# A hybrid encoder layer on one core: two gate chunks move from branch A's filler to the paired block products, and branch A's transposes and value products follow two steps later

## The chip, the core and the metric

The kernel runs on one core of a Trainium2 chip. Its engines are TensorE (PE in the profile, with weight loads as PEld), VectorE (DVE), ScalarE (ACT), GpSimd (POOL) and SyncE (SP), which here only issues DMA transfers. The metric is device microseconds (us) of one execution, as the median of several runs.

## What is computed

One encoder layer for two sequences, a prompt of 256 rows and a sample of 1024, together 1280 rows of width 1024 in float32.

```python
def _layer(x, rel_bias, g_mix, w_in, b_gate, w_branch_a, w_branch_b, w_out, sink, g_mlp, w_up, w_down):
    h = _rmsnorm(x, g_mix)
    z = h @ w_in
    # qa, ka, va | qb, kb, vb | gates: columns of z
    ...
    gates = jax.nn.sigmoid((z[..., o6:] + b_gate).astype(jnp.float32)).astype(x.dtype)
    gates = gates.reshape(b, S, 2, D_MODEL)
    o_a, _ = _banded_attention(qa, ka, va, A_WINDOW, 1, rel_bias[:, :A_HEADS], sink)
    o_b = _dilated_mixture(qb, kb, vb, rel_bias[:, A_HEADS:])
    merged = gates[:, :, 0] * (o_a.reshape(b, S, A_Q) @ w_branch_a) + gates[:, :, 1] * (o_b @ w_branch_b)
    x = x + merged @ w_out
    h = _rmsnorm(x, g_mlp)
    return x + jnp.square(jax.nn.relu(h @ w_up)) @ w_down
```

Branch A is attention in a window of 128 with 8 query heads, 2 key heads and a sink in the denominator. Branch B is a mixture of three dilated windows, weighted by a softmax over their log-sums. A final RMS norm follows the layer.

## The kernel before, in words

Every matrix product of float32 data is made of three: each operand is split in a high part (`whi`, `hhi`, made by an ACT copy) and a remainder (`wlo`, `hlo`, made by a DVE subtraction), and PE adds high × low, low × high and high × high.

The stages, in order of time. First the norm and the values' columns of `z`. Then 14 **pairs** (`PAIRS`, `pair()` L1039): two chunks of 128 columns of `w_in` are taken together, and their product with the sample's rows is made as seven products of blocks (`seven` L359) in place of eight, with the prompt's rows by a plain product (`prompt` L362). Pairs 0 to 8 run alone; pairs 9 to 13 (from `MIXED` on) run with branch B's attention beside them. The last six pairs hold gate columns, whose results are stored to DRAM (`scr_g`). Then comes **branch A's loop** (L1465), and then 48 merging **jobs** (the loop behind it), each of which multiplies branch B's or A's output with `w_branch_b` or `w_branch_a` and, on DVE, with a gate. `w_out` and the MLP end the kernel.

Branch A's loop runs over 40 tiles, four units (pairs of heads) of ten tiles of 128 rows, two tiles to a step `j`. A step of PE has, in this order: `values_of` (L1199) of the tiles four back, `transposes` (L1183) of the tiles two back, `scores` (L1160) of tile j, filler, scores of tile j+1, filler. DVE adds the bias and takes the maxima (L1170, L1174), ACT takes the exponentials (L1180), both copy the transposed weights out of PSUM (L270, L272), and DVE copies the result `o` (L1213), which SP stores.

The **filler** is the generator `logits()` (L1216). It makes the five gate chunks that are left (`PLAIN`), each as three plain products (512, 512 and 256 rows, `mm3` L188), with 24 matmuls each. It hands back control after 4 wide matmuls or 8 narrow ones; a step of the loop takes three such pieces. A result is copied by ACT (`gs`, L1227) and stored. The next chunk's weights are split (`prepare()`, `whi` L231, `wlo` L235) on the way.

Beside the loop, `merge()` (L1245) makes branch B's mixture on POOL (L1342, L1345) from rows `r` that SP loads (L1323, L1326), two items to a step. `wslot` hands out a ring of ten buffers (`N_W`) to all of `raw`, `whi`, `wlo`, `gs` and `r`; whoever takes a buffer waits for the last reader of what was there.

At the loop's end, `sums_a` (L1410 to L1413) turns the sums of exponentials into reciprocals; `rows_a` transposes them on PE (L1418), copies them (L1420) and stores them (L1422); `widen` (L1431) loads them back, spread over partitions. `fetch()` (L222) loads the next weights, `load_gate` (L1449) gates, `open_gate` (L1454) takes their sigmoid, and `high_b`, `low_b` (L1378, L1381) split branch B's output. A job's product lies in one of three PSUM banks until DVE multiplies it with its gate into `mT` (L1551).

The order of instructions on each engine is that of the code: nothing reorders them. SP issues transfers in order too, and each waits for the end of one that it issued eight before.

Of the kernel before, what the change touches and what calls it, by code (L numbers as in the profile page):

```python
# [15 lines left out]
P = 128  # L16
# [27 lines left out]
         (2, 512, 8, AH + 2 * BH, BH, 256, 127))  # L44

PAIRS = [(off + 256 * g, off + 256 * g + P) for g in (2, 1, 0) for off in (OFF_K, OFF_Q)]
PAIRS += [(0, P), (2 * P, 3 * P), (512, OFF_G)] + [(OFF_G + P * c, OFF_G + P * c + P) for c in (1, 3, 5, 7, 9)]

MIXED = 9
PLAIN = range(11, 16)  # L50
HALVES = (slice(0, HD), slice(HD, P))
ALL = {mybir.EngineType.Activation, mybir.EngineType.DVE, mybir.EngineType.PE, mybir.EngineType.Pool,
       mybir.EngineType.SP}
# [44 lines left out]
def encoder_kernel(  # L98
# [120 lines left out]
    def fetch():  # L219
        src, shape, _ = specs[len(raws)]  # L220
        raws.append(wslot("raw", shape))
        nc.sync.dma_start(raws[-1], src)  # L222
# [15 lines left out]
    def weight(ahead=None):  # L238
        i = taken[0]
        taken[0] += 1  # L240
        while len(ready) < min(len(specs), i + 1 + (AHEAD if ahead is None else ahead)):
            prepare()
        return ready[i]
# [78 lines left out]
    def steps_of(gen, n):  # L322
        for _ in range(n):
            next(gen, None)
# [126 lines left out]
    def load_bias(u, make):  # L451
        b = make("bias", (P, 2, 3 * P))
        nc.gpsimd.dma_start(b, toeplitz(0, 3 * P, -P, 2 * u))
        return b
# [690 lines left out]
    if True:  # L1145
# [4 lines left out]
        def a3(name, shape=(P, 2, 3 * P), n=3, dt=F32):  # L1150
            return att.tile(list(shape), dt, name=name, tag=name, bufs=n)
# [6 lines left out]
        live, units = {}, {}  # L1158

        def scores(u, t):  # L1160
            st, bias = units[u]
            lo, W, c0 = tiles[t]
            s = a3("s", n=3)
            m = small.tile([P, 2], F32, name="m", tag="m")
            for h in range(2):
                ps = bank("sc")
                q = st["q"][h][:, P * t : P * t + P]
                nc.tensor.matmul(ps[:, :W], q, st["k"][1][:, P * lo : P * lo + W], start=True, stop=False)
                nc.tensor.matmul(ps[:, :W], q, st["k"][0][:, P * lo : P * lo + W], start=False, stop=True)
                nc.vector.tensor_tensor_reduce(  # L1170
                    s[:, h, :W], ps[:, :W], bias[:, h, c0 : c0 + W], 1.0, -3.0e38,
                    op0=ALU.add, op1=ALU.max, accum_out=m[:, h : h + 1],
                )
            nc.vector.scalar_tensor_tensor(nm_a[:, 2 * u : 2 * u + 2, t], m, -1.0, nsink[:, 2 * u : 2 * u + 2],  # L1174
                                           op0=ALU.mult, op1=ALU.min)
            live[u, t] = s
# [191 lines left out]
    if True:  # L1368
# [5 lines left out]
        def high_b(b):  # L1374

            ob_hi.block(b)
            ob_lo.block(b)
            nc.scalar.activation(ob_hi.t[b, 0], merged[b], AF.Copy)  # L1378
# [83 lines left out]
        merges = merge()  # L1462
        next(merges)
        steps_of(fill, 2)
        for j in range(0, n + 2, 2):  # L1465
            if j > 2:
                values_of(*order[j - 4])
            if j:
                transposes(*order[j - 2])
            if j == n:  # L1470
                sums_a()
            if j < n:
                scores(*order[j])
                next(fill)
                for h in range(2):
                    exponential(*order[j], h)
                scores(*order[j + 1])
                steps_of(fill, 2)
                if j > 2:
                    steps_of(merges, 2)  # L1480
                for h in range(2):
                    exponential(*order[j + 1], h)
            else:
                steps_of(fill, 2)
                next(merges, None)
            if j == n - 4:
                high_b(0)
                low_b(0)
            if j < n and order[j][1] == 0 and order[j][0] < 3:
                u = order[j][0] + 1  # L1490
                units[u] = load_unit(u), load_bias(u, lambda name, shape: a3(name, shape, 2))
            if j in (n - 6, n - 4):
                fetch()
            if j in (n - 4, n - 2):
                load_gate(j - n + 4)
                load_gate(j - n + 5)
                load_o(j - n + 4)
        prepare()
        values_of(*order[n - 2])
        run(merges)  # L1500
        next(fill)
        prepare()
        w_bs = [weight(0), weight(0)]
        w_as = [None] * 4

        rows_a()
        widen(0)
        fetch()
        for i in range(4):
            if i < 2:  # L1510
                open_gate(i)
            next(fill)
            if i == 0:
                high_b(1)
                low_b(1)
                widen(2)
        run(fill)
        for i in range(4, 8):
            load_gate(i)
        side = {0: [(weigh, 0)], 3: [(turn_a, 0)], 4: [(low_a, 0)], 5: [(turn_a, 1)], 6: [(low_a, 1)],  # L1520
                7: [(turn_a, 2)], 8: [(low_a, 2)], 9: [(turn_a, 3)], 10: [(low_a, 3)], 11: [(high_b, 2), (low_b, 2)],
                12: [(weigh, 1)], 14: [(turn_a, 4)], 15: [(low_a, 4)], 17: [(turn_a, 5)], 19: [(low_a, 5)],
# [540 lines left out]
```

## Time and profile before

| what | us |
|---|---|
| median of 3 runs | 1670.78 (1670.15 to 1671.09) |
| the profiled execution | 1671.05 |
| its span, first to last instruction | 1669.3 |
| values and start, pairs alone, pairs beside branch B | 0 to 118.9, to 342, to 534.8 |
| branch A's loop with its tail | 534.8 to 681.0 |
| merging jobs | 681.0 to 766 |
| busy in the span: PE, DVE, ACT, POOL | 1658.3, 954.1, 715.1, 484.8 |

A row of a timeline has the start and the length of an instruction in us, its engine, line, operation, output and inputs with their shapes, a count where rows are joined, and in brackets the idle time of its engine before it with what ended it. Matmuls are pipelined: the length of one is more than the distance to the next one's start, and that distance is what it costs.

### The profile page before, as it was taken

How to read it: one execution, taken by the hardware profiler on the slowest of the kernel's cores; microseconds unless marked ns; L12 is line 12 of the kernel's file. 1: busy time of each engine (PE TensorE's matmuls, PEld its weight loads, DVE VectorE, ACT ScalarE, POOL GpSimd, SP SyncE). 2: the span in 40 equal slices, each digit the busy share in tenths (PEclk: the TensorE clock that was granted, in tenths of full speed). 3: DMA queues.
4: the chain of work that ended last, by engine and by line, in shares of the span. 5: the costliest groups of instructions: out<-in, count | busy, mean ns of one | idle time of the engine just before them, and what ended most of it. 6: DMA issues, size and time to landing. Idle time of an engine off the chain costs nothing.

```text
span 1669.3 us, 24690 instructions
## 1 busy us (share of the span) xinstructions
PE 1658.3 (99%) x9217; PEld 1410.3 (84%) x9217; DVE 954.1 (57%) x1535; ACT 715.1 (43%) x1473; POOL 484.8 (29%) x362
## 2 busy tenths in 40 slices
PE   9999999999999999999999999999999999999998
PEld 7898888888888888788888888888888888888886
DVE  6732233455654565677378455455456775867665
ACT  6232323345654565654176333333334333333435
POOL 1212222121112353000100555455554250514240
PEclk9999999999999999999999999999999999999999
DMA  7416562666667795965111443343356934733333
GB/s 257 150 53 127 135 126 78 169 185 200 187 192 220 196 236 162 254 203 202 46 81 59 161 161 125 117 161 130 113 191 235 359 115 136 253 102 108 120 121 126
DMA packets 226993, 265.11 MB, mean 159 GB/s; under 512 B 29663, under 2 KB 156511, under 8 KB 226873
## 3 DMA queue, kind: packets, MB, share of 16 engines
q1 hardware_dynamic: 219816, 245.35, 46.5%
q0 software_dynamic: 6720, 17.65, 5.3%
q8 instruction: 73, 1.20, 0.3%
q10 hardware_dynamic: 336, 0.53, 0.1%
q14 instruction: 48, 0.39, 0.1%
HBM read 177.75 MB, written 90.96 MB: 161 GB/s over the span
## 4 chain that ended last, share of the span: by engine, by line
PE 95%; DVE 2%; ACT 1%; DMA 1%; issue 0%; SPq 0%; ACTq 0%
PE dn L346 22%; PE x L346 20%; PE mm L192 13%; PE z L346 10%; PE v L820 6%; PE y L346 5%; PE mm L346 5%; PE sc L346 3%; PE pv L346 3%; PE pv L1210 2%; PE pt L1194 2%; PE sc L554 1%; PE pv L601 1%; PE pt L587 1%; PE tr L337 1%; DMA sg<-scr_g 1%
## 5 line engine op out<-in xcount | busy, mean ns | idle before, releaser
L346 PE MATMUL dn<-dhi,ulo 128*128 128x512 f32 x448 | 174.3, 389 | 0.0
L346 PE MATMUL dn<-dlo,uhi 128*128 128x512 f32 x448 | 174.3, 389 | 0.0
L346 PE MATMUL dn<-dhi,uhi 128*128 128x512 f32 x448 | 174.3, 389 | 0.0
L346 PE MATMUL x<-chi,wlo 128*128 128x512 f32 x424 | 166.5, 393 | 0.0
L346 PE MATMUL x<-clo,whi 128*128 128x512 f32 x424 | 165.6, 390 | 0.0
L346 PE MATMUL x<-chi,whi 128*128 128x512 f32 x424 | 165.0, 389 | 0.0
L313 DVE TENSOR_TENSOR wlo<-ta,whi 128x1024 fp32r<-128x1024 f32 x30 | 55.7, 1855 | 173.4 <-ACT whi L311 173.4
L392 POOL TENSOR_TENSOR tb<-raw 128x512 f32<-128x512 f32 x25 | 32.7, 1307 | 410.6 <-PE mm L192 159.2
L313 DVE TENSOR_TENSOR wlo<-raw,whi 128x1024 fp32r<-128x1024 f32 x60 | 89.7, 1496 | 103.7 <-ACT whi L311 101.0
L346 PEld LDWEIGHTS dn<-dlo,uhi 128*128 128x128 f32 x448 | 84.1, 188 | 17.5
L346 PEld LDWEIGHTS dn<-dhi,uhi 128*128 128x128 f32 x448 | 84.1, 188 | 17.4
L346 PEld LDWEIGHTS dn<-dhi,ulo 128*128 128x128 f32 x448 | 84.1, 188 | 17.3
L346 PEld LDWEIGHTS x<-chi,whi 128*128 128x128 f32 x424 | 79.6, 188 | 16.9
L346 PEld LDWEIGHTS x<-chi,wlo 128*128 128x128 f32 x424 | 79.8, 188 | 15.2
L346 PEld LDWEIGHTS x<-clo,whi 128*128 128x128 f32 x424 | 79.8, 188 | 14.6
L1755 POOL TENSOR_TENSOR t<-raw,t 128x1024 f32<-128x1024 f32 x16 | 45.7, 2870 | 148.6 <-DMA raw<-in_w_down_dram 148.5
L186 DVE TENSOR_TENSOR ulo<-uraw,uhi 128x1024 fp32r<-128x1024 f32 x56 | 86.1, 1558 | 4.5 <-ACT uhi L185 4.5
L1906 DVE TENSOR_TENSOR v<-v,dn 128x512 f32<-128x512 f32 x90 | 59.7, 683 | 40.5 <-PE dn L346 38.5
L2006 POOL TENSOR_TENSOR u<-u,u 128x640 f32<-128x640 f32 x16 | 25.1, 1570 | 179.0 <-ACT u L1924 179.0
L186 DVE TENSOR_TENSOR dlo<-raw,dhi 128x1024 fp32r<-128x1024 f32 x32 | 50.5, 1601 | 45.2 <-ACT dhi L185 44.2
L346 PE MATMUL dn<-dhi,up 128*128 128x512 f32 x224 | 73.5, 389 | 0.0
L346 PE MATMUL z<-chi,wlo 128*128 128x512 f32 x184 | 71.6, 389 | 0.0
(319 smaller groups left out, 4605.3 us busy)
## 6 DMA issues: line engine op xcount, KB each, us to landing
scr_u<-u SPq DMA_DIRECT2D x112, 320.0 KB, 2.6
uraw<-scr_u SPq DMA_DIRECT2D x56, 512.0 KB, 4.4
raw<-in_w_down_dram SPq DMA_DIRECT2D x36, 512.0 KB, 7.0
raw<-in_w_up_dram SPq DMA_DIRECT2D x32, 512.0 KB, 5.5
raw<-in_w_in_dram SPq DMA_DIRECT2D x25, 512.0 KB, 5.4
sg<-scr_g SPq DMA_DIRECT2D x32, 256.0 KB, 5.9
uraw<-scr_u SPq DMA_DIRECT2D x28, 256.0 KB, 4.4
qk<-scr_kb SPq DMA_DIRECT2D x48, 128.0 KB, 2.8
```

Source lines behind the costliest of these rows:

```text
L186: nc.vector.tensor_tensor(lo, src, hi.bitcast(F32), op=ALU.subtract)
L192: nc.tensor.matmul(ps, a, b, start=i == 0, stop=i == len(seq) - 1)
L313: nc.vector.tensor_tensor(lo, src, hi.bitcast(F32), op=ALU.subtract)
L337: nc.tensor.transpose(ps[:, P * i : P * (i + 1)], xn[t][:, P * k : P * (k + 1)], ident)
L346: nc.tensor.matmul(ps, a, b, start=first and i == 0, stop=last and i == len(seq) - 1, skip_group_check=True)
L392: (nc.vector if vector else nc.gpsimd).tensor_tensor(o, x, y, op=ALU.subtract)
L820: nc.tensor.matmul(ps[:, :n], a, b, start=k == 0 and j == 0, stop=k == KC - 1 and j == 2)
L1194: nc.tensor.transpose(ps[:, P * k : P * k + P], s[:, h, P * b : P * b + P], ident)
L1210: nc.tensor.matmul(pv[HALVES[h], P * i : P * i + P], src, pt[:, at + 2 * b + h, :], start=b == 0, stop=b == W // P - 1, skip_group_check=True)
L1755: nc.gpsimd.tensor_tensor(o, a, b, op=ALU.subtract)
L1906: nc.vector.tensor_tensor(v, v, ps, op=ALU.add)
L2006: nc.gpsimd.tensor_tensor(u[S1], u21, u22, op=ALU.add)
```

## The change

`PAIRS` gets one pair more, the gate chunks 11 and 12, and `PLAIN` loses them: 13, 14 and 15 are left as filler. `MIXED` moves from 9 to 10, so that five pairs still run beside branch B, and ten alone. In the loop, transposes follow their scores two steps later rather than one, and values three rather than two, in a loop that is one step longer; a step takes two pieces of filler rather than three. Scores get four buffers rather than three, and a unit's bias one buffer or, for unit 2, one of the ring. The splitting of `w_branch_b`, `high_b`, `low_b` and the row sums' turn move in among the loop's last steps, and the last values go to the end.

```diff
-PAIRS += [(0, P), (2 * P, 3 * P), (512, OFF_G)] + [(OFF_G + P * c, OFF_G + P * c + P) for c in (1, 3, 5, 7, 9)]
-
-MIXED = 9
-PLAIN = range(11, 16)
+PAIRS += [(0, P), (2 * P, 3 * P), (512, OFF_G)] + [(OFF_G + P * c, OFF_G + P * c + P) for c in (1, 3, 5, 7, 9, 11)]
+
+MIXED = 10
+PLAIN = range(13, 16)
...
-            s = a3("s", n=3)
+            s = a3("s", n=4)
...
-        for j in range(0, n + 2, 2):
+        for j in range(0, n + 4, 2):
+            if j > 4:
+                values_of(*order[j - 6])
             if j > 2:
-                values_of(*order[j - 4])
-            if j:
-                transposes(*order[j - 2])
+                transposes(*order[j - 4])
             if j == n:
                 sums_a()
...
-                steps_of(fill, 2)
+                next(fill, None)
                 if j > 2:
                     steps_of(merges, 2)
                 for h in range(2):
                     exponential(*order[j + 1], h)
-            else:
-                steps_of(fill, 2)
-                next(merges, None)
-            if j == n - 4:
+            if j == n - 2:
                 high_b(0)
                 low_b(0)
             if j < n and order[j][1] == 0 and order[j][0] < 3:
                 u = order[j][0] + 1
-                units[u] = load_unit(u), load_bias(u, lambda name, shape: a3(name, shape, 2))
-            if j in (n - 6, n - 4):
+                units[u] = load_unit(u), load_bias(u, wslot if u == 2 else lambda name, shape: a3(name, shape, 1))
+            if j in (n - 8, n - 6):
                 fetch()
+            if j in (n - 4, n - 2):
+                prepare()
+            if j == n:
+                w_bs = [weight(0), weight(0)]
+                rows_a()
+                widen(0)
+                next(merges, None)
+                next(fill, None)
+                fetch()
+                for i in range(2):
+                    open_gate(i)
             if j in (n - 4, n - 2):
                 load_gate(j - n + 4)
                 load_gate(j - n + 5)
                 load_o(j - n + 4)
-        prepare()
-        values_of(*order[n - 2])
         run(merges)
-        next(fill)
-        prepare()
-        w_bs = [weight(0), weight(0)]
         w_as = [None] * 4
-
-        rows_a()
-        widen(0)
-        fetch()
-        for i in range(4):
-            if i < 2:
-                open_gate(i)
-            next(fill)
-            if i == 0:
-                high_b(1)
-                low_b(1)
-                widen(2)
+        high_b(1)
+        low_b(1)
+        widen(2)
         run(fill)
         for i in range(4, 8):
             load_gate(i)
+        values_of(*order[n - 2])
```

What the engines get from it is seen in their order of instructions. The first place is PE at the end of branch A, around the transpose of the row sums (`tn`, L1418); `pv` are value products, `pt` transposes, and `mm<-h..,w..` filler. Before:

```order
L192 MATMUL mm<-hhi,whi 128x512
L192 MATMUL mm<-hhi,wlo 128x512
L1210 MATMUL pv<-pt,vp 64x128 x8
L192 MATMUL mm<-hlo,whi 128x512
L192 MATMUL mm<-hhi,whi 128x512
L192 MATMUL mm<-hhi,wlo 128x512
L192 MATMUL mm<-hlo,whi 128x512
L1418 MATMUL tn<-ident,l_a 80x128
L192 MATMUL mm<-hhi,whi 128x512
```

And in the changed kernel, from the last two filler matmuls behind the last scores on:

```order
L192 MATMUL mm<-hlo,whi 128x512
L192 MATMUL mm<-hhi,whi 128x512
L1210 MATMUL pv<-pt,va 64x128 x12
L1194 MATMUL pt<-ident,s 128x128 x10
L1418 MATMUL tn<-ident,l_a 80x128
L192 MATMUL mm<-hhi,wlo 128x512
L192 MATMUL mm<-hlo,whi 128x512
L192 MATMUL mm<-hhi,whi 128x512
L192 MATMUL mm<-hhi,wlo 128x512
L1210 MATMUL pv<-pt,va 64x128 x10
L1194 MATMUL pt<-ident,s 128x128 x8
```

The turn of the row sums moved ahead of two groups of value products, one of transposes and most of the filler that stood before it.

The second place is DVE at the same point: the last maxima (`nm_a<-m,nsink`), the copies `o` and `pt`, the row sums (L1410 to L1420) and the remainders `wlo` and `oblo` of weights and of branch B's output. Before:

```order
L1174 SCALAR_TENSOR_TENSOR nm_a<-m,nsink 128x2
L1213 COPY o<-pv 128x256
L272 COPY pt<-pt 128x512
L1410 TENSOR_TENSOR nm_a<-nm_a,nsink 128x80
L1412 TENSOR_TENSOR l_a<-l_a,nm_a 128x80
L1413 RECIPROCAL l_a<-l_a 128x80
L235 TENSOR_TENSOR wlo<-raw,whi 128x1024
L1213 COPY o<-pv 128x256
L235 TENSOR_TENSOR wlo<-raw,whi 128x1024
L1420 COPY o<-tn 80x128
```

And in the changed kernel:

```order
L1174 SCALAR_TENSOR_TENSOR nm_a<-m,nsink 128x2
L1381 TENSOR_TENSOR oblo_0_7087<-merged,obhi_0_7086 128x1024
L235 TENSOR_TENSOR wlo<-raw,whi 128x1024
L1213 COPY o<-pv 128x256
L272 COPY pt<-pt 128x512
L1410 TENSOR_TENSOR nm_a<-nm_a,nsink 128x80
L1412 TENSOR_TENSOR l_a<-l_a,nm_a 128x80
L1413 RECIPROCAL l_a<-l_a 128x80
L1420 COPY o<-tn 80x128
```

One remainder of branch B's output and one of the weights now stand between the last maxima and the row sums, and none between the reciprocal and the copy of its transpose.

The third place is DVE in step 22 of the loop, with the buffers' numbers. Before, the weights' remainder of the last filler chunk but one stood behind the maxima of both tiles of step 24:

```order
L1174 SCALAR_TENSOR_TENSOR nm_a_5347<-m_6426,nsink_77 128x2
L1170 ISA s_6446,m_6447<-sc_6448,bias_5858 128x384
L1170 ISA m_6447 128x1
L1170 ISA s_6446,m_6447<-sc_6452,bias_5858 128x384
L1170 ISA m_6447 128x1
L1174 SCALAR_TENSOR_TENSOR nm_a_5347<-m_6447,nsink_77 128x2
L235 TENSOR_TENSOR wlo_6461<-raw_6190,whi_6460 128x1024
L1213 COPY o_6500<-pv_6487 128x256
```

In the changed kernel that of the last filler chunk stands between the two tiles of step 22:

```order
L1170 ISA s_6431,m_6432<-sc_6437,bias_5988 128x384
L1170 ISA m_6432 128x1
L1174 SCALAR_TENSOR_TENSOR nm_a_5534<-m_6432,nsink_77 128x2
L235 TENSOR_TENSOR wlo_6446<-raw_6048,whi_6445 128x1024
L1170 ISA s_6456,m_6457<-sc_6458,bias_5988 128x384
L1170 ISA m_6457 128x1
L1174 SCALAR_TENSOR_TENSOR nm_a_5534<-m_6457,nsink_77 128x2
```

It moved from the end of a step into the middle of one, ahead of the second tile's maxima; its buffer was that of the rows of POOL's product `merged_6384<-r_6293`, the first of the second merged block.

## The prediction

> **What bounds the kernel now.** I read the page's engine shares first, then its chain, then the table of what TensorE (PE) waited for, then the stages as windows.
>
> ```profile
> PE 1658.3 (99%) x9217; PEld 1410.3 (84%) x9217; DVE 954.1 (57%) x1535; ACT 715.1 (43%) x1473; POOL 484.8 (29%) x362
> PE 95%; DVE 2%; ACT 1%; DMA 1%; issue 0%; SPq 0%; ACTq 0%
> PE mm L192 <- DVE mT L1551: 1.5, 2, 1.1
> 534.80:681.00 146.20, 146.20 (x1146) 126.71 (x1146) 85.59 (x269) 84.41 (x224) 57.21 (x64) 1.00 0.73 198
> 681.00:766.00 85.00, 83.51 (x434) 71.24 (x433) 63.63 (x109) 49.77 (x98) 0.00 (x0) 1.00 0.81 255
> ```
>
> PE is busy 99% of the span and is 95% of the chain. In branch A's loop (fourth row: window, its length, then busy PE, weight load, DVE, ACT, POOL, granted clock, DMA share) it is busy for all 146.20 us. In the merging jobs (fifth row) it loses 1.5 us, in the two waits of the third row. So a matmul removed anywhere is worth its full start-to-start time, and a wait added to PE costs its full length: nothing behind it has slack to take it back. Two things are thus to be worked out: how much PE work goes, and whether A, with less filler, still covers everything else.
>
> **The pair: −3.0 us.** Two gate chunks leave the filler.
>
> ```profile
> 143.73:168.57 24.84, 24.84 (x134) 21.52 (x133) 8.02 (x7) 6.95 (x10) 6.14 (x5) 1.00 0.53 121
> 591.14 0.40 PE L192 MATMUL mm<-hhi,wlo 128*128 128x512 f32 x1
> 592.75 0.39 PE L192 MATMUL mm<-hlo,whi 128*128 128x512 f32 x1
> 672.69 0.28 PE L192 MATMUL mm<-phi,wlo 128*128 128x256 f32 x1
> 675.44 0.28 PE L192 MATMUL mm<-phi,whi 128*128 128x256 f32 x1
> ```
>
> Between the second and third row lie seven starts: 1.61/7 = 0.230 us for a 512-wide matmul in the loop; between the last two lie 23: 2.75/23 = 0.120 us for a 256-wide one. A chunk has 48 and 24 of them: 48 × 0.230 + 24 × 0.120 = 13.9, two 27.8. The pair that replaces them costs one period of the pairs stage, 24.84 us, in which DVE, ACT and POOL are busy a third of the time, the DMA share is 0.53 and PE never stops (first row); its weight fetches, its sums and the stores of its gates lie beside it and cost nothing. 27.8 − 24.84 = 3.0 saved. Were that cover gone it would show as PE waits in that window; nothing there comes near it.
>
> **The wait before the row sums' turn: +4.2 us.** After the last scores, the change puts PE's transpose of the row sums (L1418) directly behind the ten transposes of step 36.
>
> ```profile
> 658.72 0.39 PE L192 MATMUL mm<-hlo,whi 128*128 128x512 f32 x1
> 659.04 1.53 PE L1210 MATMUL pv<-pt,va 128*64 128x128 f32 x24
> 660.50 1.31 PE L1194 MATMUL pt<-ident,s 128*128 128x128 f32 x10
> 661.57 0.36 PE L1168 MATMUL sc<-kp,qp 128*128 128x256 f32 x1
> 663.41 0.28 PE L1169 MATMUL sc<-kp,qp 128*128 128x256 f32 x1
> ...
> 664.31 0.16 DVE L1174 SCALAR_TENSOR_TENSOR nm_a<-m,nsink 128x2 f32<-128x2 f32 x1
> ...
> 659.14 1.04 ACT L1378 ACTIVATE obhi<-merged 128x1024 fp32r<-128x1024 f32 x1
> 664.76 0.50 ACT L1180 ACTIVATE s<-s,nm_a 128x256 f32<-128x256 f32 x1
> 665.26 0.50 ACT L1180 ACTIVATE s<-s,nm_a 128x256 f32<-128x256 f32 x1
> ...
> 660.21 1.23 DVE L1381 TENSOR_TENSOR oblo<-merged,obhi 128x1024 fp32r<-128x1024 f32 x1 [2.17 <-ACT obhi L1378]
> 661.35 0.42 DVE L1213 COPY o<-pv 128x256 f32<-128x256 f32 x1
> 661.69 0.68 DVE L272 COPY pt<-pt 128x512 f32<-128x512 f32 x1
> 662.28 0.41 DVE L1170 CUSTOM_DVE_ANT_0 s<-sc,bias 128x256 f32<-128x256 f32 x1
> 668.53 0.23 DVE L1410 TENSOR_TENSOR nm_a<-nm_a,nsink 128x80 f32<-128x80 f32 x1
> 669.10 0.24 DVE L1412 TENSOR_TENSOR l_a<-l_a,nm_a 128x80 f32<-128x80 f32 x1 [0.34 <-ACT nm_a L1411]
> 669.37 0.65 DVE L1413 RECIPROCAL l_a<-l_a 128x80 f32<-128x80 f32 x1
> 670.05 1.23 DVE L235 TENSOR_TENSOR wlo<-raw,whi 128x1024 fp32r<-128x1024 f32 x1
> ```
>
> Count from the last scores matmul (663.41). PE in the new order: 0.1, four filler matmuls 0.9 and a hitch of 0.1, values 1.46 (659.04 to 660.50), ten transposes 1.07 (660.50 to 661.57): at L1418 after 3.6 us. What L1418 needs: maxima done at +1.06 (664.31 + 0.16), two exponentials 1.0, then ACT's obhi, 1.07 until DVE's oblo can start (659.14 to 660.21), and on DVE, in its order, oblo 1.14, wlo 1.14 (same shape), o 0.34, pt 0.59, and the sums 0.57 + 0.27 + 0.68 (668.53 to 670.05): 7.8. PE stands 4.2 us. In the kernel before, the same chain is met by 12 filler matmuls and 16 value products more, and without oblo and wlo ahead: L1418 shows no wait (its row stands below). Queued behind it on PE is everything; bounds 3.5 (both exponentials overlapped with the maxima) and 6.0 (a late DMA ahead of whi).
>
> The granted clock is 1.00 in every window quoted, and no wait in them passes 1.1 us. The Trainium skill, TensorE: Matmul & The Clock Gate, section "Part 1: The HAM clock gate", says that PE falls to half its clock after an idle free-running window of about 3.4 us and needs as long at work to come back. By that rule this wait alone could bring the gate into play, for about 1.7 us more (an estimate by that page); no run here shows it yet.
>
> **The wait at the fourth merging job: +2.5 us.** Jobs 0 to 2 fill the three PSUM banks; job 3 needs the bank that DVE's mT empties, and mT stands on DVE behind wlo of the first w_a piece, whose fetch SP issues behind the row sums' store and broadcast.
>
> ```profile
> 671.65 0.27 PE L1418 MATMUL tn<-ident,l_a 128*80 128x128 f32 x1
> 672.65 0.28 DVE L1420 COPY o<-tn 80x128 f32<-80x128 f32 x1
> 681.03 0.39 PE L192 MATMUL mm<-obhi,wlo 128*128 128x512 f32 x1
> 682.69 1.06 ACT L231 ACTIVATE whi<-raw 128x1024 fp32r<-128x1024 f32 x1 [0.25 <-DMA raw<-in_w_branch_a_dram]
> 684.88 0.39 PE L192 MATMUL mm<-obhi,whi 128*128 128x512 f32 x1
> 685.66 0.50 PE L192 MATMUL mm<-obhi,wlo 128*128 128x512 f32 x1 [0.39 <-DVE mT L1551]
> 703.39 0.50 PE L192 MATMUL mm<-obhi,wlo 128*128 128x512 f32 x1 [1.09 <-DVE mT L1551]
> ```
>
> L1418 to job 3 took 685.66 − 671.65 = 14.0; L1420 waited about 0.7 behind another wlo, which now stands earlier: 13.3. PE's work between them shrinks: 12 filler matmuls 2.8, 36 value products 2.2 and 8 transposes 0.9 (both scaled from the rows above), 18 matmuls of jobs 0 to 2 4.1 (681.03 to 684.88, and one more), hitches 0.3: 10.3. Wait 3.0 for 0.55 now (684.88 + 0.23 to 685.66): +2.5, between 1.0 (a quicker fetch) and 3.5. The second wait (703.39) hangs on gate loads queued on SP; as jobs come later after those loads' start it shrinks, I take −0.7 of 1.3, bounds −1.3 and 0.
>
> **The ring in A: +2.0 us.** Filler weights, gate copies and branch B's rows share ten buffers. The filler now reaches its last chunk's wlo in step 22, mid-iteration, in a buffer that POOL's product for the second merged block must leave first.
>
> ```profile
> 593.07 1.53 PE L1210 MATMUL pv<-pt,va 128*64 128x128 f32 x24
> 605.78 1.09 PE L1210 MATMUL pv<-pt,vp 128*64 128x128 f32 x16
> ...
> 609.37 1.30 POOL L1342 TENSOR_TENSOR merged<-r 128x512 f32<-128x512 f32 x1 [3.52 <-DMA r<-scr_c]
> ...
> 570.00:640.00 70.00, 70.00 (x568) 60.39 (x567) 44.43 (x140) 40.48 (x114) 37.95 (x34) 1.00 0.91 230
> ```
>
> That product ended 17.6 us after step 18 began (593.07 to 610.67). Step 22 will begin 12.7 − 2 × 0.92 = 10.9 after it, and DVE comes to wlo some 4 later: it waits 2.7, of which about 1.9 is slack before PE asks for the next scores bank: 0.8. But the rows came by DMA at a share of 0.91: six iterations shortened by 0.92 each give 5.5 us, and the queues can give back only 9% of 39, 3.5, so they fall 2.0 further behind: 2.8. I take 2.0, nearer the second because POOL's row shows it waiting for DMA; bounds 0 and 5. Also, wlo of the first w_b piece now stands ahead of step 38's maxima: +0.5 (0 to 1.5: two exponentials' length behind its wlo at one end).
>
> **Edits at nothing.** The later transposes and values are the same instructions with more lead; a fourth scores buffer gives them room. The bias of a unit is asked for ten tiles ahead; its one buffer is read last two units earlier, and unit 2's stands in the ring. PE's 146.20 of 146.20 covers such loads now; were one late by an iteration, it would show as a scores matmul that waits, at up to 5 us each. Stores of o go out a step later on SP, among loads that nobody on PE waits for within a step; the row sums' store and broadcast pass the last two o stores, which is part of the chain of 13.3 above.
>
> **Sum:** −3.0 + 4.2 + 2.5 − 0.7 + 2.0 + 0.5 = +5.5. The profiled run took 1671.05 (its span 1669.3 and 1.75 around it), 0.27 above the median 1670.78; 1671.05 + 5.5 − 0.27 = 1676.3.
>
> **Rivals.**
> - *Gain.* Each iteration loses 0.09 at the turn to values (658.72 to 659.04, against 0.23). If that is a wait for ACT's pt copies rather than a switch, two steps of lead remove it: 19 × 0.09 = 1.7. With the pair and the shorter second wait: −5.4. It decides if the two new waits and the ring stay under 2.1 together. For: PE was never seen short in A. Against: the chain of 7.8 against 3.6. Time about 1667, mostly under the bound. Chance 0.11.
> - *Little change.* The waits come at their low ends (3.5, 1.0, ring 0): +0.3 to +2.5, 1671 to 1673.5. For: transfers that left earlier land earlier. Chance 0.23.
> - *Ring worse.* DMA at 0.91 makes gate copies on ACT late too, and exponentials stand behind them: ring 5 to 7, 1680 to 1682. For: POOL's 3.52 wait. Chance 0.12.
> - *Clock.* By the mechanism told above, the wait of 4.2 halves the clock for about 3 us: 1.7 more, 1678. Against: the idle time exceeds one such window by little, so alignment is needed. That page's rule makes no other difference. Chance 0.08.
> - That the change does not do what it says: the order of the built program, shown with the change, says that it does; no chance is kept for it.
>
> **How the numbers follow.** Forecast 0.46, with its own range 1673.5 to 1679. A measurement tells 0.2%, about 3.3 us: faster is under 1667.4, slower over 1674.1. Faster 0.09 from the gain; same 0.26 (little change, the rest of the gain and a little of the forecast's low end); slower 0.65. The range 1668.5 to 1682 leaves out under 2 in 10: half the gain and the worst of the ring.
>
> **What would show it.** Among PE's waits, L1418 behind DVE's L1413 with 3.5 to 6 us, and job 3's matmul behind mT with 1.0 to 3.5; a pairs stage 24.84 longer; A's loop shorter by 27.8 less those waits; DVE's wlo in step 22 idle before it on POOL or ACT. Wrong would be: L1418 without a wait (then the gain), PE idle in many iterations of A (then lead or buffers are short, which I price at nothing), or a granted clock under 1.00.

## The result, and the profile after

| | before | after |
|---|---|---|
| time, median (range, runs), us | 1670.78 (1670.15 to 1671.29, 6) | 1681.34 (1680.18 to 1682.72, 6) |
| profiled execution, us (its span) | 1671.05 (1669.3) | 1681.73 (1680.0) |

The changed kernel takes 1.0064 of the time before, 95% interval 1.0051 to 1.0077: slower by 10.6 us in the medians and by 10.7 in the profiled executions. The page's engine shares and chain say little (PE still 99%); what PE waited for says where to look (what waits, on what; us in all, times, longest):

```profile
PE 1660.2 (99%) x9205; PEld 1411.6 (84%) x9205; DVE 957.0 (57%) x1540; ACT 717.5 (43%) x1475; POOL 493.7 (29%) x366
PE 93%; DMA 3%; ACT 2%; DVE 2%; issue 0%; SPq 0%; POOL 0%; DVEq 0%; ACTq 0%; POOLq 0%
PE sc L1168 <- DVE m L1170: 4.5, 2, 4.2
PE tn L1418 <- DVE l_a L1413: 4.1, 1, 4.1
PE mm L192 <- DVE mT L1546: 1.8, 2, 1.6
```

Of these three kinds, before had the third alone, with 1.5 us. Two long waits are new: 4.2 us at a scores matmul inside branch A's loop and 4.1 us at the transpose of the row sums. The windows of the changed kernel show what the waits alone don't (window, length, busy PE, weight load, DVE, ACT, POOL, then the granted clock, DMA share, GB/s):

```profile
342.20:367.04 24.84, 24.84 (x135) 21.52 (x134) 6.92 (x7) 6.95 (x10) 9.75 (x8) 1.00 0.54 151
...
624.87:628.28 3.41, 0.97 (x9) 0.73 (x7) 0.03 (x1) 1.45 (x3) 3.08 (x3) 1.00 1.10 238
628.28:635.10 6.82, 5.09 (x14) 4.61 (x15) 6.75 (x16) 3.56 (x11) 5.22 (x5) 0.50 0.87 175
635.10:679.48 44.38, 43.66 (x385) 37.36 (x384) 27.88 (x91) 30.37 (x84) 15.54 (x16) 1.00 0.68 204
679.48:682.89 3.41, 0.00 (x0) 0.00 (x0) 2.98 (x7) 1.52 (x4) 0.00 (x0) 1.00 0.25 91
682.89:686.30 3.41, 3.10 (x15) 2.29 (x17) 0.45 (x2) 1.84 (x3) 0.00 (x0) 0.50 0.05 12
686.30:700.00 13.70, 13.51 (x84) 10.72 (x81) 9.15 (x15) 7.91 (x13) 0.00 (x0) 1.00 0.96 296
```

The first row is the added pair: 24.84 us with PE busy throughout, the length it was priced at. The others, which begin and end where the granted clock changes or 3.41 us ahead of its falls, hold the loss. At each of the two waits the granted clock falls to 0.50, from 628.28 to 635.10 and from 682.89 to 686.30, and it is 1.00 in the other rows. So each wait is paid twice, once while PE stands and once while it works at half speed.

The first wait, in the timeline of the changed kernel (start, duration, engine, line; in brackets the idle time ahead and what ended it):

```profile
610.39 1.28 POOL L1342 TENSOR_TENSOR merged<-r 128x512 f32<-128x512 f32 x1 [14.28 <-DMA r<-scr_c]
...
625.28 1.52 POOL L1345 TENSOR_TENSOR merged<-merged,r 128x512 f32<-128x512 f32 x1
626.76 1.27 POOL L1342 TENSOR_TENSOR merged<-r 128x512 f32<-128x512 f32 x1
...
626.83 0.38 ACT L1227 ACTIVATE gs<-mm 128x256 f32<-128x256 f32 x1 [6.36 <-POOL merged L1345]
627.11 1.05 ACT L231 ACTIVATE whi<-raw 128x1024 fp32r<-128x1024 f32 x1
...
628.25 1.23 DVE L235 TENSOR_TENSOR wlo<-raw,whi 128x1024 fp32r<-128x1024 f32 x1 [5.90 <-ACT whi L231]
629.39 0.55 DVE L1170 CUSTOM_DVE_ANT_0 s<-sc,bias 128x384 f32<-128x384 f32 x1
...
624.52 1.31 PE L1194 MATMUL pt<-ident,s 128*128 128x128 f32 x10
630.01 0.69 PE L1168 MATMUL sc<-kk,q 128*128 128x384 f32 x1 [4.17 <-DVE m L1170]
...
631.45 0.63 PE L192 MATMUL mm<-hhi,whi 128*128 128x512 f32 x1
631.88 0.63 PE L192 MATMUL mm<-hhi,wlo 128*128 128x512 f32 x1
```

Read backwards from PE's wait: the maxima that free the scores bank stand on DVE behind wlo, wlo waits for whi, whi stands on ACT behind the gate copy of the filler chunk before it, and that copy wants a ring buffer whose rows POOL is still adding (until 626.80). POOL had itself waited 14.28 us for its first rows by DMA (10.56 before). It did not fall behind, though: counted from the loop's first scores (561.46; 536.76 before), its sum ended at 65.3 us, 3.8 sooner than before. But with less filler PE would have come to the scores of step 24 at 64.4 us, 13.7 sooner than before. The last two rows start 0.43 us apart, where 512-wide matmuls are 0.230 apart at full clock.

The second wait, in the same kernel and view:

```profile
673.91 0.39 PE L192 MATMUL mm<-hlo,whi 128*128 128x512 f32 x1
674.67 0.38 PE L1168 MATMUL sc<-kp,qp 128*128 128x256 f32 x1 [0.37 <-DVE m L1170]
...
677.82 1.31 PE L1194 MATMUL pt<-ident,s 128*128 128x128 f32 x10
683.20 0.40 PE L1418 MATMUL tn<-ident,l_a 128*80 128x128 f32 x1 [4.07 <-DVE l_a L1413]
...
694.85 0.39 PE L192 MATMUL mm<-obhi,whi 128*128 128x512 f32 x1
695.43 0.50 PE L192 MATMUL mm<-obhi,wlo 128*128 128x512 f32 x1 [0.19 <-DVE mT L1546]
...
713.70 0.50 PE L192 MATMUL mm<-obhi,wlo 128*128 128x512 f32 x1 [1.65 <-DVE mT L1546]
...
676.02 0.16 DVE L1174 SCALAR_TENSOR_TENSOR nm_a<-m,nsink 128x2 f32<-128x2 f32 x1
678.29 1.23 DVE L1381 TENSOR_TENSOR oblo<-merged,obhi 128x1024 fp32r<-128x1024 f32 x1 [2.11 <-ACT obhi L1378]
679.43 1.22 DVE L235 TENSOR_TENSOR wlo<-raw,whi 128x1024 fp32r<-128x1024 f32 x1
...
682.40 0.65 DVE L1413 RECIPROCAL l_a<-l_a 128x80 f32<-128x80 f32 x1
```

From these rows the difference of the two profiled executions adds up:

| term | us | worked out |
|---|---|---|
| the pair | −3.0 | 24.84 as priced; the two chunks as priced |
| scores wait in step 24 | +4.4 | 624.52 + 1.07 for ten transposes, to 630.01 |
| half clock behind it | +2.6 | 630.01 to 635.1, halved |
| L1418 | +4.3 | 677.82 + 1.07, to 683.20 |
| half clock behind it | +1.5 | 683.20 to 686.3, halved |
| fourth merging job | −0.2 | 694.85 + 0.23 to 695.43 is 0.35, for 0.55 before |
| second wait on mT | +0.55 | 1.65 for 1.09 |
| step 38, behind wlo | +0.5 | 673.91 + 0.23 to 674.67 |
| sum | +10.65 | +10.7 between the profiled executions |

The two terms of the clock are estimates: by starts 0.43 us apart in place of 0.230, rather than by halving, they would be 2.4 and 1.4.

### The profile page after: what moved, and what is told of

Its sections match the earlier page's. It is cut to its first block, busy times and chain, and to the rows that moved or that the text cites. A ratio compares the mean times of both kernels' runs of the same rounds, so it can differ in the third digit from the quotient of the medians.

```text
span 1680.0 us, 24628 instructions
## 1 busy us (share of the span) xinstructions
PE 1660.2 (99%) x9205; PEld 1411.6 (84%) x9205; DVE 957.0 (57%) x1540; ACT 717.5 (43%) x1475; POOL 493.7 (29%) x366
## 4 chain that ended last, share of the span: by engine, by line
PE 93%; DMA 3%; ACT 2%; DVE 2%; issue 0%; SPq 0%; POOL 0%; DVEq 0%; ACTq 0%; POOLq 0%
PE dn L346 22%; PE x L346 20%; PE mm L192 11%; PE z L346 10%; PE v L820 6%; PE mm L346 5%; PE y L346 5%; PE sc L346 3%; PE pv L346 3%; PE sc L554 1%; PE pv L601 1%; PE pt L587 1%; PE pt L1194 1%; PE pv L1210 1%; DMA sg<-scr_g 1%; DMA wl<-scr_l 1%
## 5 line engine op out<-in xcount | busy, mean ns | idle before, releaser
L346 PE MATMUL x<-chi,wlo 128*128 128x512 f32 x436 | 171.2, 393 | 0.0
L346 PE MATMUL x<-clo,whi 128*128 128x512 f32 x436 | 170.2, 390 | 0.0
L346 PE MATMUL x<-chi,whi 128*128 128x512 f32 x436 | 169.7, 389 | 0.0
L346 PEld LDWEIGHTS dn<-dhi,uhi 128*128 128x128 f32 x448 | 84.1, 188 | 17.6
L346 PEld LDWEIGHTS x<-chi,wlo 128*128 128x128 f32 x436 | 82.1, 188 | 15.6
```

Source lines behind the costliest of these rows:

```text
L346: nc.tensor.matmul(ps, a, b, start=first and i == 0, stop=last and i == len(seq) - 1, skip_group_check=True)
```

## The experiments

All twelve runs were timed beside the kernel before on the same chip (its medians there 1670.7 to 1671.2). The first four take the change apart; the others ask whether the pair's 3.0 us can be had with other tails or another spread of the filler. Their diffs are against the changed kernel where nothing else is said.

**Merging two iterations later.** If the first wait comes from the ring, then a later start of branch B's merging, which changes the order in which its rows and the filler take the ring's buffers, should remove it.

```diff
-                if j > 2:
+                if j > 6:
                     steps_of(merges, 2)
```

> The changed kernel, with branch B's merging begun two steps of the loop later (from step 8 rather than 4); nothing else. Theory T (the scores in step 24 wait because ACT's gate copy and DVE's weight remainder wait for ring buffers that POOL still reads, and the granted clock falls behind that wait of 4.2 us): the wait at L1168 and the slow matmuls after it go, the clock stays 1.00 in that stretch, about 4.4 + 2.6 = 7.0 us less, 1674.3. Rival D (POOL and the transfers are late by themselves, and moving their place in the order only moves the wait): a wait of like size in a later step, 1680 to 1682. Rival C (the clock falls for a reason of its own, not behind the wait): the wait goes and the slow stretch stays, 1677. The wait at L1418 stays at 4 us in all of them.

Measured 1675.01 (1673.94 to 1677.49), ratio 1.0027 (1.0019 to 1.0036). The waits of PE and the windows of this run:

```profile
PE tn L1418 <- DVE l_a L1413: 4.1, 1, 4.1
PE sc L1168 <- DVE m L1170: 0.7, 1, 0.7
600.00:660.00 60.00, 60.00 (x526) 52.09 (x525) 41.84 (x135) 38.21 (x110) 37.65 (x34) 1.00 0.78 194
671.30:674.71 3.41, 1.54 (x16) 1.13 (x12) 2.73 (x4) 2.34 (x4) 0.00 (x0) 1.00 0.64 208
674.71:681.54 6.83, 4.64 (x27) 3.50 (x27) 2.05 (x6) 2.89 (x4) 0.00 (x0) 0.50 0.30 95
629.36 1.54 POOL L1345 TENSOR_TENSOR merged<-merged,r 128x512 f32<-128x512 f32 x1
```

The 4.2 us are gone, and with them the half clock: 60.00 of 60.00 at 1.00. That is 6.3 us of the changed kernel's time, near the two terms' 7.0; against the gain stands L1418's spell of half clock, which is now twice as long (6.83 us; why is told in the last section). POOL's last sum for the first merged block ends even later here (last row: 630.90, for 626.80), and yet nothing waits for it. So the first wait is the ring's, as the order of merges and filler makes it, and neither POOL's lateness by itself nor the lead of two steps, which this run keeps.

**The row sums behind the last transposes.** The row sums' turn, with their store and broadcast, leaves the loop's last pass and follows it; the fetch of w_a thereby goes ahead of their store on SP.

```diff
             if j == n:
                 w_bs = [weight(0), weight(0)]
-                rows_a()
-                widen(0)
                 next(merges, None)
...
                 load_o(j - n + 4)
+        rows_a()
+        widen(0)
         run(merges)
```

> The changed kernel, with the row sums' transpose, its store and broadcast moved behind the last group of transposes (four filler matmuls, 20 value products and 8 transposes later on PE), so that the fetch of the first w_a piece goes ahead of them on SP. Theory T: the wait at L1418 falls from 4.1 to about 1.1 us, the clock stays 1.00 behind it, and job 3 waits no more: 3.2 + 1.4 + 0.3 = 4.9 us less, 1676.4. Rival M (the chain behind the row sums only moves: job 3 then waits for its weights by 3 us or more): 1679 to 1681. Rival C (clock of its own): 1678. The wait in step 24 stays.

Measured 1679.17 (1677.59 to 1689.07), ratio 1.0056 (1.0036 to 1.0077); its profiled execution was the slowest of its runs (its granted clock stood at 0.50 from 10.7 to 24.3 us, long before the loop), and only its waits are read here:

```profile
PE mm L192 <- DVE mT L1546: 4.9, 3, 2.2
PE sc L1168 <- DVE m L1170: 4.6, 2, 4.2
PE pv L1210 <- DVE o L1213: 1.1, 1, 1.1
```

L1418's wait is gone and a gain of 2.2 us remains where 4.3 and 1.5 had stood and 4.9 had been expected: the rest moved to the merging jobs (mT 4.9 for 1.8) and the value products. The jobs' waits begin at the eighth job, behind gates for which ACT waits 6.0 us, and not at the fourth behind the weights. The first wait is untouched, so the two don't hang together.

**Both edits.** The two diffs above together.

> Both of the edits before it in one kernel. Theory T: 7.0 + 4.9 = 11.9 us less than the changed kernel, 1669.4, that is the pair's saving of 3.0 less some 1.6 of small waits: faster than the kernel before by 1 to 2 us, clock 1.00 throughout. Rivals D or M: one of the waits is left, 1674 to 1680.

Measured 1675.18 (1673.64 to 1679.73), ratio 1.0025 (1.0017 to 1.0034): no better than the merging alone. The 1669.4 that had been expected was missed, and so was the 1672.8 that the two measured gains would give together. What PE and ACT waited for, by their timelines, and one window:

```profile
691.28 0.50 PE L192 MATMUL mm<-obhi,wlo 128*128 128x512 f32 x1 [1.60 <-DVE mT L1546]
704.68 0.50 PE L192 MATMUL mm<-obhi,wlo 128*128 128x512 f32 x1 [2.12 <-DVE mT L1546]
...
688.12 1.40 ACT L1454 ACTIVATE sg<-sg,bg 128x512 f32<-128x512 f32 x2 [5.87 <-DMA sg<-scr_g]
...
705.00:709.00 4.00, 4.00 (x17) 3.54 (x16) 3.32 (x8) 2.25 (x6) 0.00 (x0) 0.57 0.99 292
```

PE now reaches the merging jobs at 679.9, for 685.3 with the merging alone; the gates' transfers are not there yet, and a wait of only 2.12 us is followed by half clock for 3.4 us (4 us at a mean of 0.57).

**The lead alone.** The kernel before with the later transposes and values, the fourth scores buffer and the change's bias buffers, but with its own chunks and tail. Against the kernel before:

```diff
-            s = a3("s", n=3)
+            s = a3("s", n=4)
...
+            if j > 4:
+                values_of(*order[j - 6])
             if j > 2:
-                values_of(*order[j - 4])
-            if j:
-                transposes(*order[j - 2])
+                transposes(*order[j - 4])
```

> The kernel before, with transposes one step later and values one step later, four scores buffers and the bias as in the change; pairs, filler and tail as before. Theory T (the lead costs and brings nothing by itself, since PE is never short in the loop): 1670.8 within 1 us, no wait on PE over 1.5 us. Rival H (each turn to value products hid a wait of 0.09 us): 1669. Rival L (the lead itself, by its buffers, makes the waits of the changed kernel): over 1674.

Measured 1671.02 (1669.98 to 1674.48), ratio 1.0002 (0.9994 to 1.0011): no change. Its loop shows no new wait; in the merging jobs the longest is 2.2 us, for 1.1 before and at most 1.5 expected. So the lead itself, and the buffers it needs, cost and bring nothing that the times show while the filler is whole.

**The tail of before, the filler thinned in the loop.** The pair, the lead and the later merging; the second filler piece of a step only in every other step, and what is left of it behind the loop, in the tail of before.

```diff
-                next(fill, None)
-                if j > 2:
+                if j % 4 == 0:
+                    next(fill)
+                if j > 6:
                     steps_of(merges, 2)
```

> The kernel before with the pair and the lead of the change, but with its own tail: a step of the loop takes a second piece of filler only every other time, so that 13 pieces are left behind the last scores as before, the row sums' turn stands where it stood, and branch B's merging begins at step 8. Theory T2 (what the change lost beside the ring is the filler behind the last scores, which covers the row sums' chain, the first w_a piece and the gate loads): no wait at L1418, waits for mT within 2.5 us, clock 1.00 in the loop, 1668 to 1669, faster than the kernel before by 2 to 3 us. Rival S (steps with one piece of filler are too short for DVE and ACT): waits at the scores over 3 us in all, 1671 or more. Rival P (a pair costs more than its period shows, so that there is no gain to be had): 1670.8 without any new wait.

Measured 1680.12 (1677.29 to 1681.04), ratio 1.0049 (1.0035 to 1.0062). The profiled execution, 1677.29, was the fastest of the five. In it the tail is clean, the loop isn't. PE's waits, and ACT's timeline:

```profile
PE sc L1168 <- DVE m L1170: 7.5, 4, 3.8
PE mm L192 <- DVE mT L1554: 0.5, 1, 0.5
641.89 0.38 ACT L1227 ACTIVATE gs<-mm 128x256 f32<-128x256 f32 x1 [4.10 <-DMA r<-scr_c]
```

The gate copy on ACT waits again, this time for a merged row's transfer that holds the ring's next buffer. The prediction for the tail held, that for the loop missed.

**The same with before's lead.** As the last, with transposes and values one step earlier, three scores buffers and the bias buffers, as before. Against the last:

```diff
-            if j > 4:
-                values_of(*order[j - 6])
             if j > 2:
-                transposes(*order[j - 4])
+                values_of(*order[j - 4])
+            if j:
+                transposes(*order[j - 2])
```

> The same with the lead of the kernel before: transposes one step behind their scores, three scores buffers. Theory N (the lead is not needed, PE has enough beside the scores): within 1 us of the run with the lead. Theory Y (with less filler a step, the transposes would wait for ACT's exponentials; that is what the lead is for): waits at L1194 or L1210 on ACT in the steps with one piece, 0.3 to 1 us in each of ten, 3 to 10 us more.

Measured 1685.81 (1682.35 to 1687.87), ratio 1.0083 (1.0066 to 1.0100). A new wait appears, at the transposes:

```profile
PE pt L1194 <- ACT s L1180: 8.1, 13, 3.8
```

Thirteen transposes wait for exponentials. The longest of these waits, 3.8 us, is the ring's again (ACT's whi waited 3.27 us for a buffer that POOL still read, and the exponentials stood behind it); the other twelve come to 4.3. Here lies the use of the lead: in this spread of the filler it is worth 5.7 us, and nothing while the filler is whole.

**Other places for the filler that is left.** Three runs have the tail of before, the lead and the later merging, and differ in which steps get a second piece; a fourth takes the changed kernel's filler with its tail in another order.

```diff
                 if 10 <= j <= 32:
                     next(fill)
```

> The run that kept the tail's filler and the lead, with the second piece of filler in steps 10 to 32, where branch B's rows are loaded, and one piece in the steps before and behind them; merging from step 8 on. Theory R (the waits at the scores in that run came from short steps while the transfers of the rows fill the queues): they fall from 7.5 to under 2 us, tail without new waits, 1669 to 1671. Rival S (steps with one piece are too short wherever they stand): as before it, 1678 to 1680.

Measured 1683.79 (1682.7 to 1685.16), ratio 1.0075 (1.0061 to 1.0088): worse, with 10.9 us at scores in four waits, the longest 6.1.

```diff
                 if j < 32:
                     next(fill)
```

> The run that kept the tail, with the loop's pace as in the changed kernel up to step 30 (two pieces a step) and one piece in the last four steps, so that seven pieces of filler are left behind the last scores; merging from step 8 on. Theory RT (two separate costs: chunk ends that fall among the loads of branch B's rows, and too little filler behind the last scores; here the first is as in the run with later merging, which had no such wait, and half of the second is given back): no wait over 1.5 us in the loop, none at L1418, waits for mT 2 to 4 us, 1669 to 1672. Rival S (steps with one piece are too short wherever they stand): waits at the scores in steps 32 to 38, 1673 or more.

Measured 1676.40 (1674.17 to 1677.08), ratio 1.0029 (1.0018 to 1.0040): the loop has only 1.5 us left, but seven pieces behind it no longer reach, and the fourth job waits 5.5 us where 2 to 4 had been expected.

```diff
                 if j < 26:
                     next(fill)
```

> The same with one piece in the last seven steps, so that ten pieces are left. Theory RT: waits for mT at most 2.5 us, 1668.5 to 1671; by it not slower than the run with seven. Rival S: slower than the run with seven by 1 us or more, with waits at the scores.

Measured 1675.25 (1671.29 to 1677.36), ratio 1.0025 (1.0013 to 1.0036). Ten pieces behind the loop, and the same wait, where at most 2.5 us had been expected. Its waits, and ACT's timeline:

```profile
PE mm L192 <- DVE mT L1554: 5.7, 1, 5.7
PE sc L1168 <- DVE m L1170: 1.9, 1, 1.9
687.80 1.06 ACT L231 ACTIVATE whi<-raw 128x1024 fp32r<-128x1024 f32 x1 [6.85 <-DMA raw<-in_w_branch_a_dram]
```

It is the piece of w_a that comes late, asked for behind the row sums' store and broadcast on SP. More cover on PE doesn't help a transfer that starts when PE has got so far.

The fourth merges later too, and puts w_a's fetch and the last gate loads ahead of the row sums on SP, and the row sums and the second piece of w_b behind the loop:

```diff
             if j == n:
-                w_bs = [weight(0), weight(0)]
-                rows_a()
-                widen(0)
...
+                high_b(0)
+                low_b(0)
                 fetch()
-                for i in range(2):
-                    open_gate(i)
+                for i in range(4, 8):
+                    load_gate(i)
...
+        rows_a()
+        w_bs = [weight(0), weight(0)]
+        widen(0)
```

> The changed kernel with the merging from step 8 on, and its tail in another order: branch B's first remainder and the second w_b piece behind the row sums on DVE, the row sums' transpose behind the last transposes on PE, and the first w_a piece and four gate loads ahead of the row sums' store and broadcast on SP. Amount and place of the filler as in the change. Theory T3 (the tail's waits come from the order on DVE and SP, not from the amount of filler): no wait at L1418, waits for mT at most 2.5 us, clock 1.00 nearly throughout, 1668.5 to 1670.5, below the kernel before. Rival F (too little filler behind the last scores, whatever the order): waits of 4 us or more in all somewhere between the row sums and job 9, 1672 to 1676.

Measured 1675.19 (1673.72 to 1677.18), ratio 1.0027 (1.0017 to 1.0038): no wait at L1418, but 6.8 us on mT in four. With the changed kernel's little filler behind the last scores, the jobs' transfers have too little beside them in each of the orders of the tail that were tried.

**The w_a fetch first.** The run with second pieces up to step 24, with w_a's fetch ahead of the row sums on SP, and the split of branch B's first output block (`high_b`, `low_b`) behind them. Against that run:

```diff
-            if j == n - 4:
-                high_b(0)
-                low_b(0)
...
+        fetch()
         rows_a()
+        high_b(0)
+        low_b(0)
         widen(0)
-        fetch()
```

> The run with ten pieces left, with the first w_a piece fetched ahead of the row sums' store and broadcast on SP, and branch B's first remainder behind the row sums on DVE. There PE stood 5.7 us at job 3 for that piece, whose fetch left SP 8 us after the row sums' transpose, and 1.9 us at the scores of step 38 behind that remainder. Theory K (these two waits and the slow clock behind them are all that the pair's saving still lacks): both gone, waits for mT at most 2.5 us, clock 1.00 throughout, 1667.5 to 1669.5, faster than the kernel before by 1.5 to 3.5 us. Rival G (the gate loads and the broadcast take the place, as they did in the run with the tail reordered and the change's own filler): waits for mT of 4 us or more, 1672 to 1675.

Measured 1673.55 (1671.62 to 1675.78), ratio 1.0013 (1.0003 to 1.0023): the nearest to the kernel before, 7.8 us below the changed one. The gain of 1.5 to 3.5 us over the kernel before that had been expected did not come. Its waits, ACT's timeline and two windows:

```profile
PE mm L192 <- DVE mT L1553: 4.2, 2, 3.1
688.26 1.40 ACT L1454 ACTIVATE sg<-sg,bg 128x512 f32<-128x512 f32 x2 [7.72 <-DMA sg<-scr_g]
690.00:700.00 10.00, 8.59 (x32) 6.99 (x33) 9.43 (x19) 7.87 (x16) 0.00 (x0) 0.83 1.08 292
690.00:730.00 40.00, 37.55 (x179) 31.43 (x180) 32.04 (x61) 25.52 (x52) 0.00 (x0) 0.96 1.05 311
```

Now the gates are late, and PE's 3.1 us stand at the eighth job. In the profiled execution the terms nearly close: 4.2 for the 1.5 of before, half of the 3.4 us at half clock (1.7), less the 3.0 saved: +1.4, of 1.7 between the spans (1671.0 and 1669.3).

Then the same with the last four gate loads ahead of the row sums as well:

```diff
         fetch()
+        for i in range(4, 8):
+            load_gate(i)
         rows_a()
...
-        for i in range(4, 8):
-            load_gate(i)
```

> The run with the first w_a piece fetched early, with the loads of the gates of jobs 4 to 7 also ahead of the row sums' store and broadcast on SP. There ACT stood 7.7 us for a gate and PE 3.1 us at job 3 behind it. Theory K (order on SP is what is left, with ten pieces of filler to cover the broadcast): waits for mT at most 2.5 us, clock 1.00, 1669 to 1671, not slower than the kernel before. Rival G (the transfers of the tail take their time in any order, and the next of them is waited for): waits for mT of 3 us or more in all, 1672 to 1674.

Measured 1674.73 (1672.64 to 1677.12), ratio 1.0024 (1.0014 to 1.0035): with these gates ahead, the broadcast of the row sums is late (DVE waits 3.7 us for it) and then later jobs' gates, and mT waits 6.6 us in three. In the run before it the DMA share is 1.05 over the 40 us in which the jobs run (last row above). In the kernel before it is as high, 1.06 over the first 40 us of its jobs, with waits of only 1.5 us; but there PE has 17.6 us of work between the last scores and the first job, and here 15.6. With the queues full, of the tail's transfers whichever was put last was the one waited for, in each of these runs.

No version beat the kernel before. Whether any order keeps the pair's 3.0 us stays open.

## Why the prediction was right in its direction and short in its size

The time lies 5.0 us above the 1676.3 of the sum, outside the forecast's own range (to 1679), and 0.7 inside the outer one (to 1682). That it stayed inside is in part luck, since errors of the terms cancelled (below). The time is also that of the rival "ring worse" (1680 to 1682, chance 0.12), and its mechanism, gate copies late on ACT, is what the trace shows (PE's wait came from there by way of whi and wlo, not of the exponentials); but the ring cost 4.4 us and not 5 to 7, and the clock, which that rival did not have, made up the number.

- **The pair, −3.0.** Right, by the window of 24.84.
- **L1418, +4.2.** Right: 4.07 waited, 4.3 from the transposes' end. DVE's order and lengths (oblo, wlo, o, pt, sums) are the predicted ones, and moving the turn away removed the wait.
- **The ring, +2.0.** The mechanism was right: branch B's rows, for which POOL waits on DMA, hold a buffer that the filler wants, and merging later ends it. The step named for it was not the one: the late instruction was the gate copy on ACT behind POOL's last sum for the first merged block, and wlo followed it. The product that the prediction named, the first of the second block, came right behind that sum and ended at 628.03, so by its reading wlo could have begun at most 0.2 us sooner (628.25). This term was mis-sized: 4.4 for 2.0, within its bounds of 0 to 5. The prediction let the queues give back 3.5 of 5.5 us by which PE would come sooner; counted from the loop's first scores, POOL's sum came 3.8 sooner and step 24 of PE 13.7.
- **Step 38, +0.5.** Right, 0.5.
- **The fourth job, +2.5.** Wrong: −0.2. From L1418 to that job took 12.2 us rather than 13.3 (683.20 to 695.43), and PE's work between took 11.9 rather than 10.3, of which 1.5 is the half clock. PE was slow enough to arrive late. This is a loss that covered a loss. That the fourth job's wait would come out without it was not shown: in the second experiment w_a's fetch goes first as well, and the jobs' 4.9 us stand at later ones.
- **The second wait on mT, −0.7.** Wrong in sign, +0.55. Counted from the first job, the first gate loads went out 1.1 us sooner than before, as forecast, but one of the later ones landed 0.9 us later (23.1 for 22.2); why was not followed up.
- **The clock.** The step that failed is the pricing of a wait at its own length. The sum had no term for what the clock does behind it; it stood as a rival of 0.08 and 1.7 us, at one wait. It came at both, with 2.6 and 1.5 us. The Trainium skill, TensorE: Matmul & The Clock Gate, section "Part 1: The HAM clock gate", which was weighed there, gives half clock after an idle window of about 3.4 us, until as long a time at work; the trace agrees in the state (0.50) and in the length (3.4 and 6.8 us), and differs in that about half of such a window idle was enough (below).
- **Edits at nothing.** The lead, the buffers, the bias and the stores were priced right: the kernel with these alone is the same as before.

By terms: the ring 2.4 over its estimate, the clock 4.1, L1418 0.1, the jobs −2.7 and +1.25: 5.15 over the 5.5 predicted. The fourth job's error thus hid a third of the others' 7.85.

The larger cause, seen only with the twelve runs: 28 us of filler were not only work on PE. They were the time in which two chains of transfers (branch B's rows through the shared ring, and the row sums, weights and gates of the first merging jobs) went by unseen. The 3.0 us saved on PE were lost again in each of the orders tried. In the best of them the added waits came to 2.7 us, less than the saving, and the half clock behind one of them (1.7) made it a loss.

## What to carry to other kernels

Where PE is busy all the time, work moved out of a stage takes its cover along: list the transfers that run beside it, and price the change by the chain that becomes the longest in that stage, not by the matmuls saved. Price a wait of some 3 us or more on PE at its length plus 1.7 us, or 3.4 where the clock stays down for a second period; which of the two it is hangs on where the wait falls (next section). A longer lead is worth trying only together with less filler, since each of the two alone shows nothing or a loss.

## What the runs showed of the hardware

In the stages from 340 to 800 us the granted clock fell to 0.50 for 3.4 or for 6.8 us, never for another length, and long waits of PE set it off. From the waits of PE over 1.4 us in the stages from 340 to 800 us of all profiled runs:

| one wait of PE, us | spells of half clock behind it |
|---|---|
| up to 1.65 (1.49, 1.50, 1.51, 1.60, 1.65) | none of 5 |
| 1.71 to 2.54 | 3 of 9 (1.71, 2.12 and 2.25; not 1.74, 1.82, 1.86, 2.20, 2.21 and 2.54), and one after a pair of 2.39 and 2.21 close together |
| 2.76 to 6.1 | all of 12 (2.76, 3.13, 3.29, 3.76, 3.77, 4.05, 4.07, 4.17, 4.22, 5.47, 5.73, 6.1) |

Of the twelve, five were followed by 6.8 us (4.05, 4.17, 5.47, 5.73, 6.1) and seven by 3.4, the waits of 4.07 and 4.22 among these.

Why waits of one length differ can be read from the same traces. In each of the 14 profiled executions all changes of the granted clock lie a whole multiple of 3.413 us apart (62 changes, to within 0.02 us), whatever the program does there. So the time is divided into windows of 3.413 us that run on regardless of the program. Sorted by the time in a window in which no matmul ran, the windows from 340 to 800 us give:

| clock in a window | PE idle in it, us | clock in the window behind it |
|---|---|---|
| 1.00 | up to 1.68 (1831 windows) | 1.00 in all |
| 1.00 | 1.71 to 1.82 (6) | 0.50 in one (1.71), 1.00 in five |
| 1.00 | 1.87 to 3.41 (15) | 0.50 in all |
| 0.50 | up to 0.51 (16) | 1.00 in all |
| 0.50 | 1.43 to 3.41 (5) | 0.50 in all |

So what counted was whether PE stood idle for about half of one window, and not the length of the wait as such. L1418 shows it: its 4.07 us in the changed kernel filled one window (679.48 to 682.89) and left 0.31 us in the next, and the clock was down for one. Its 4.05 us with the merging later were split over two, 1.87 and 2.18, and the clock was down for two. By this table a wait of up to about 3.6 us (twice 1.82, an estimate) could pass at full clock where two windows share it evenly, so that all the waits from 2.76 us on were followed by half clock is in part chance. One window at half clock takes 0.001 off the mean granted clock of a run, and the six runs of the changed kernel lie between 0.995 and 0.997, which would fit waits that fall differently in the windows from run to run. No run moves one wait through a window on purpose, and between 0.51 and 1.43 us of idle time the return to full clock was not seen either way.
